# Retention with key blocks of 128, 128, 128, 112 and 32: the last block's three products of high and low parts stacked into one contraction of 96 rows

## The chip, the cores and the metric

The kernel runs on one core of one Trainium2 chip. The metric is the device time of one execution in microseconds (us), of which the median of three runs is given. TensorE (PE) does the matmuls, and PEld is its weight load; VectorE (DVE) and ScalarE (ACT) move and split numbers; GpSimd (POOL) and SyncE (SP) issue most of the transfers.

## The reference, cut to what matters

A decoder of two layers: each is a half-step SwiGLU block, a mixer, and another half-step SwiGLU block, on 16 learned tokens and 512 inputs (528 positions of width 1024). The mixer of layer 0 is retention with four heads, keys of 256 and values of 512:

```
q = rotary(q); k = rotary(k) * 256 ** -0.5
scores = einsum('bhid,bhjd->bhij', qi, ki) * decay_intra      # inside a chunk of 64
o = einsum('bhij,bhjv->bhiv', scores, vi) + einsum('bhid,bhdv->bhiv', qi * decay_q, S)
S = S * decay_chunk + einsum('bhjd,bhjv->bhdv', ki * decay_k, vi)
o = rmsnorm(o, head_norm) * silu(g)
return o @ w_out
```

Everything is in float32. The kernel computes the recurrence as one triangular product over all 528 positions: the decay is folded into the tables that turn q and k, so that scores times values with a causal mask gives the same o.

## The kernel before, in words

A float32 product is made of three matmuls. Each operand is split into a high part, rounded for the fast float32 matmul (fp32r), and a low part, which is what the rounding left. `mm3` (L397) issues high x high, high x low and low x high into one accumulator; these are the lines L398, L399 and L400 of the profile. Weights stream in by DMA and are split as they arrive: ACT makes the high part (`whi`, L159), DVE the low part (`wlo`, L160). `unit` steps do the projections, with three names of accumulators (`X..`, `QZ..`, `su..`).

Retention (`retention`, L1072) goes head by head (h = 0 to 3). After the projections of queries, keys and values, the positions are cut along the keys into NJ = 5 blocks of widths JW, 128 four times and 16. For each block j, `steps` calls two functions:

- `score(j)`: the scores of the block's keys against all later queries. The keys of the block are the matmul's weights (128 x JW), the queries are what streams past, for two halves m of the key width: 6 matmuls per block (12 for block 0, which goes in two segments). DVE multiplies the diagonal square by the causal mask (L1241), and ACT and DVE split the scores into `ph` and `pl` (L431, L432).
- `turn(j)`: four transposes on PE bring the values of the block (`vt`) into a PSUM bank `tv`, keys on partitions (L1221); ACT and DVE split them into `vh` and `vl` (L431 and L432, and L550 and L551 in head 0, where they are scaled as well).

`pv` (L1273) multiplies: for each of four value slices m an accumulator `po` collects `mm3` of every block j, with the block's values as the weights (JW rows, 128 columns) and its scores streaming. Block 4 of `po` has 16 contraction rows and 16 streaming columns. Afterwards ACT squares `po` (L1292) and DVE takes it into the gate (L1326) or, in head 3, into `ob` (L1346). Two `po` are in use at a time (pool `acc`, two buffers); scores of blocks 0 to 3 use the same pool. `tv`, the scores of block 4 and the accumulators `X..` share a ring of four banks.

In heads 0 to 2 two gate units (`Xrg..`) stand between `steps` and `pv`; in head 3 `pv` follows `steps` directly. What stands in which order on an engine is set by a scheduler that reorders by its own estimates; the engines then run their rows strictly in that order, and a row whose input is not there holds up all that stand behind it on its engine.

Of the kernel before, what the change touches and what calls it, by code (L numbers as in the profile page):

```python
# [10 lines left out]
F32 = mybir.dt.float32  # L11
F32R = mybir.dt.float32r
# [4 lines left out]
P = 128  # L17
# [5 lines left out]
MR = 32  # L23
T = 528
# [18 lines left out]
NMASK = 5  # L43

NJ = 5
JW = (128, 128, 128, 128, 16)
PO = (0, 528, 928, 1200, 1344, 1360)


BY_JT = ((0, 128, 4, 512), (512, 16, 1, 16))  # L50
# [167 lines left out]
def trunk(ctx, tc, a):  # L218
    nc = tc.nc
    V, S, G = nc.vector, nc.scalar, nc.gpsimd  # L220

    const = ctx.enter_context(tc.tile_pool(name="const", bufs=1))
# [129 lines left out]
    ident = const.tile([P, P], F32, name="ident")  # L352
    nc.sync.dma_start(ident, a["tri"][0])
    causal = const.tile([P, P], F32, name="causal")
    nc.sync.dma_start(causal, a["tri"][1])
    ones_r = const.tile([P, P], F32R, name="ones")
    V.memset(ones_r.bitcast(F32), 1.0)
    ones = ones_r.bitcast(F32)
# [12 lines left out]
    rb = upool.tile([P, T], F32, tag="rb", name="rb")  # L371
# [13 lines left out]
    def hook():  # L385

        W.fetch()
        if pend:
            pend[0][0] -= 1
            if pend[0][0] <= 0:  # L390
                pend.popleft()[1]()
# [5 lines left out]
    def mm3(ps, lh, ll, rh, rl, start, stop, **kw):  # L397
        nc.tensor.matmul(ps, lhsT=lh, rhs=rh, start=start, stop=False, **kw)  # L398
        nc.tensor.matmul(ps, lhsT=lh, rhs=rl, start=False, stop=False, **kw)  # L399
        return nc.tensor.matmul(ps, lhsT=ll, rhs=rh, start=False, stop=stop, **kw)  # L400
# [9 lines left out]
    def acc_tile(name):  # L410
        other["turn"] += 1
        if other["banks"] == 2 and other["turn"] % 3 == 0:
            return other["pool"].tile([P, 2, 512], F32, tag="acc", name=name)
        return acc.tile([P, 2, 512], F32, tag="acc", name=name)

    def bank(name):
        if other["ring"]:
            other["ring"].rotate(-1)
            return other["pool"].tile([P, 512], F32, tag=other["ring"][-1], name=name)
        return other["pool"].tile([P, 512], F32, tag="bank", name=name, bufs=other["banks"])  # L420
# [9 lines left out]
    def split(hi, lo, src):  # L430
        S.copy(hi, src)  # L431
        V.tensor_sub(lo, src, hi.bitcast(F32))  # L432
# [116 lines left out]
    def split_scaled(hi, lo, src, by_row):  # L549
        S.activation(hi, src, AF.Copy, scale=by_row)  # L550
        V.scalar_tensor_tensor(lo, src, by_row, hi.bitcast(F32), ALU.mult, ALU.subtract)  # L551
# [520 lines left out]
    def retention(feed):  # L1072
        with tc.tile_pool(name="retp", bufs=1) as rp, tc.tile_pool(name="wmore", bufs=2) as wp, psum_pool(4) as pp:
# [40 lines left out]
            def head(h):  # L1114
                qk = {}
# [64 lines left out]
                vt, sgs, v, sc_parts = [], [], [], []  # L1180
# [34 lines left out]
                def turn(j):  # L1215
                    if not v:
                        v.extend(rp.tile([P, NJ, RDV], F32R, tag="v" + i, name=f"v{i}{h}") for i in "hl")
                    j0, jw = j * P, JW[j]
                    tv = bank(f"tv{h}{j}")
                    for m in range(4):  # L1220
                        nc.tensor.transpose(tv[:jw, m * P:(m + 1) * P], vt[m][:, j0:j0 + jw], ident)  # L1221
                    if h == 0:
                        split_scaled(v[0][:jw, j, :], v[1][:jw, j, :], tv[:jw, :], rc[:jw, j:j + 1])
                    else:
                        split(v[0][:jw, j, :], v[1][:jw, j, :], tv[:jw, :])

                def score(j):

                    if not sc_parts:
                        sc_parts.extend(rp.tile([P, PO[-1]], F32R, tag="p" + i, name=f"p{i}{h}") for i in "hl")  # L1230
                    j0, jw = j * P, JW[j]
                    sc = acc_tile(f"sc{h}{j}") if j < NJ - 1 else bank(f"sc{h}{j}").unsqueeze(1)
                    segs = HALVES if j == 0 else ((j0, T),)
                    n = segs[0][1] - segs[0][0]
                    for b, (i0, i1) in enumerate(segs):
                        for m in range(2):
                            kh, kl = qk["k", m]
                            qh, ql = qk["q", m]
                            mm3(sc[:jw, b, :n], kh[:, j0:j0 + jw], kl[:, j0:j0 + jw], qh[:, i0:i1], ql[:, i0:i1],
                                m == 0, m == 1)  # L1240
                    V.tensor_mul(sc[:jw, 0, :jw], sc[:jw, 0, :jw], causal[:jw, :jw])  # L1241
                    dst = [t[:jw, PO[j]:PO[j + 1]].rearrange("p (b t) -> p b t", b=len(segs)) for t in sc_parts]
                    split(dst[0], dst[1], sc[:jw, :len(segs), :n])

                def steps():
                    for j in range(NJ):
                        score(j)
                        turn(j)
# [24 lines left out]
                def pv(into):  # L1273

                    sqs = tmp.tile([P, T], F32, tag="sqa", name=f"osq{h}", bufs=1)
                    for m in range(4):
                        po = acc_tile(f"po{h}{m}")
                        for j in range(NJ):
                            j0, jw = j * P, JW[j]
                            for hf, (r0, r1) in enumerate(((0, P), (P, T))):  # L1280
                                i0 = max(r0, j0)
                                if i0 >= r1:
                                    continue
                                c = slice(PO[j] + i0 - j0, PO[j] + r1 - j0)
                                mm3(po[:, hf, i0 - r0:r1 - r0], v[0][:jw, j, m * P:(m + 1) * P],
                                    v[1][:jw, j, m * P:(m + 1) * P], sc_parts[0][:jw, c], sc_parts[1][:jw, c],
                                    j == 0, j == (NJ - 1 if hf else 0))
                        hook()
                        t = sqs if m == 0 else tmp.tile([P, T], F32, tag="sg", name=f"osq{h}{m}")
                        for hf, r in enumerate(((0, P), (P, T))):  # L1290
                            o = po[:, hf, :r[1] - r[0]]
                            S.activation(t[:, r[0]:r[1]], o, AF.Square)  # L1292
                            into(m, o, r)
                        if m:
                            V.tensor_add(sqs, sqs, t)
                    return sqs
# [23 lines left out]
                if h < RH - 1:  # L1320
# [4 lines left out]
                    def into(m, o, r):  # L1325
                        V.scalar_tensor_tensor(sgs[m][:, r[0]:r[1]], o, gain(m), sgs[m][:, r[0]:r[1]],  # L1326
                                               ALU.mult, ALU.mult)

                    sqs = pv(into)
                    result()  # L1330

# [8 lines left out]
                else:  # L1340
# [4 lines left out]
                    def into(m, o, r):  # L1345
                        V.tensor_scalar(ob[m][:, r[0]:r[1]], o, gain(m), None, ALU.mult)  # L1346

                    sqs = pv(into)
                    result()

# [696 lines left out]
```

## Time and profile before

| | |
|---|---|
| median of 3 runs | 2074.59 us (2074.48 to 2075.45) |
| span of the profiled execution | 2072.5 us |
| PE busy | 2061.5 us, 99% |
| DVE busy | 1789.9 us, 86% |
| ACT busy | 1192.8 us, 58% |
| POOL busy | 209.3 us, 10% |
| granted TensorE clock, mean | 0.999 |

The profile gives a span, from the first instruction to the last, and not the time of the same execution with what lies around it: the median of the runs is 2.1 us above this span. In rows of the timeline the columns are start, duration of one or of a merged group, engine, line, operation, and output from inputs. PE rows overlap, since matmuls are pipelined: what a matmul costs is the distance from its start to the start of the next one, not its duration. A form such as 16\*128 16x16 is a weight tile of 16 rows and 128 columns and an operand of 16 rows that streams 16 columns.

### The profile page before, as it was taken

Reading aid. Unit: us, or ns where it says so; the run is one execution under the profiler, and the core shown is the slowest. Engines: PE = TensorE matmul, PEld = TensorE weight load, DVE = VectorE, ACT = ScalarE, POOL = GpSimd, SP = SyncE. Lnnn points to the kernel's source line nnn. Section 1 sums busy time; section 2 is a strip of 40 time slices with the busy share of each in tenths; the row PEclk is TensorE's granted clock in tenths of the full one; section 3 lists DMA queues with packets and bytes.
Section 4 is the critical chain, followed back from the end, with each engine's and each line's share of the span. In section 5 each row is a group of like instructions: output and inputs, shape, how many; then the busy total and the mean of one; then the engine's idle time right before and its main releaser. Section 6 shows DMA issues by size and latency. Waiting matters only on the chain. (4 is left out here: it accounts for less than half of the span.)

```text
span 2072.5 us, 42971 instructions
## 1 busy us (share of the span) xinstructions
PE 2061.5 (99%) x16367; PEld 2016.6 (97%) x16367; DVE 1789.9 (86%) x3214; ACT 1192.8 (58%) x2330; POOL 209.3 (10%) x181
## 2 busy tenths in 40 slices
PE   9999999999999999999999999999999999999998
PEld 9999999999999999999999999999999988999998
DVE  8989889968686879988889998889997968998886
ACT  5656566554545455656566565666655445666664
POOL 1011111010101000111111011110101000111110
PEclk9999999999999999999999999999999999999999
DMA  7676767354554531776776376676614341686762
GB/s 223 159 190 162 193 179 193 98 144 132 144 133 131 142 101 67 183 188 161 187 194 179 107 180 181 151 208 172 200 57 117 93 162 60 166 210 175 183 178 72
DMA packets 176111, 318.84 MB, mean 154 GB/s; under 512 B 17568, under 2 KB 40736, under 8 KB 175904
## 3 DMA queue, kind: packets, MB, share of 16 engines
q1 hardware_dynamic: 133856, 237.04, 34.0%
q0 software_dynamic: 40896, 75.51, 22.4%
q10 hardware_dynamic: 1152, 3.55, 0.5%
q8 instruction: 128, 2.10, 0.4%
q14 instruction: 79, 0.65, 0.1%
HBM read 311.76 MB, written 4.26 MB: 152 GB/s over the span
## 5 line engine op out<-in xcount | busy, mean ns | idle before, releaser
L159 ACT CAST whi<-raw 128x512 fp32r<-128x512 f32 (+1 forms) x893 | 526.0, 606 | 484.3 <-DVE raw L165 97.3
L160 DVE TENSOR_TENSOR wlo<-raw,whi 128x512 fp32r<-128x512 f32 (+1 forms) x893 | 583.8, 669 | 143.4 <-ACT whi L159 136.1
L159 ACT CAST whi<-pair 128x512 fp32r<-128x512 f32 (+1 forms) x304 | 183.5, 604 | 119.5 <-PE Xf11u L399 7.3
L160 DVE TENSOR_TENSOR wlo<-pair,whi 128x512 fp32r<-128x512 f32 (+1 forms) x304 | 202.0, 665 | 7.0 <-ACT whi L159 5.6
L128 POOL DMA_DIRECT2D pair<-in_f_in x73 | 88.5, 1213 | 720.7 <-DVE wlo L160 338.7
L165 DVE TENSOR_TENSOR raw<-pair,raw 128x512 f32<-128x512 f32 (+1 forms) x146 | 97.3, 667 | 2.6
L167 DVE TENSOR_TENSOR raw<-raw,raw 128x512 f32<-128x512 f32 (+1 forms) x146 | 97.2, 666 | 2.4
L128 POOL DMA_DIRECT2D pair<-in_f_out x44 | 53.2, 1208 | 380.4 <-DVE wlo L160 133.6
L399 PE MATMUL po_r<-ogl,whi 128*128 128x264 f32 x256 | 72.7, 284 | 0.0
L398 PE MATMUL po_r<-ogh,whi 128*128 128x264 f32 x256 | 72.6, 283 | 0.0
L400 PE MATMUL po_r<-ogh,wlo 128*128 128x264 f32 x256 | 72.5, 283 | 0.0
L128 POOL DMA_DIRECT2D pair<-in_ret_in x20 | 24.3, 1216 | 297.2 <-DVE wlo L160 144.3
L398 PE MATMUL Xf20o<-hf,whi 128*128 128x264 f32 x176 | 50.9, 289 | 0.2
L398 PE MATMUL Xf11o<-hf,whi 128*128 128x264 f32 x176 | 50.9, 289 | 0.2
L398 PE MATMUL Xf10o<-hf,whi 128*128 128x264 f32 x176 | 50.8, 289 | 0.2
L399 PE MATMUL Xf10o<-hf,whi 128*128 128x264 f32 x176 | 50.0, 284 | 0.0
L399 PE MATMUL Xf11o<-hf,whi 128*128 128x264 f32 x176 | 50.0, 284 | 0.0
L399 PE MATMUL Xf20o<-hf,whi 128*128 128x264 f32 x176 | 50.0, 284 | 0.0
L400 PE MATMUL Xf20o<-hf,wlo 128*128 128x264 f32 x176 | 49.9, 285 | 0.0
L400 PE MATMUL Xf11o<-hf,wlo 128*128 128x264 f32 x176 | 49.9, 285 | 0.0
L400 PE MATMUL Xf10o<-hf,wlo 128*128 128x264 f32 x176 | 49.9, 285 | 0.0
L400 PEld LDWEIGHTS po_r<-ogh,wlo 128*128 128x128 f32 x256 | 48.2, 188 | 0.0
(987 smaller groups left out, 8523.9 us busy)
## 6 DMA issues: line engine op xcount, KB each, us to landing
raw<-in_f_in SPq DMA_DIRECT2D x277, 256.0 KB, 4.4
pair<-in_f_in SPq DMA_DIRECT2D x150, 256.0 KB, 4.7
pair<-in_f_in POOLq DMA_DIRECT2D x73, 512.0 KB, 6.4
raw<-in_f_out SPq DMA_DIRECT2D x80, 256.0 KB, 3.7
raw<-in_ret_in SPq DMA_DIRECT2D x76, 256.0 KB, 3.0
raw<-in_f_out SPq DMA_DIRECT2D x72, 192.0 KB, 3.0
pair<-in_f_out SPq DMA_DIRECT2D x48, 256.0 KB, 3.8
pair<-in_f_out POOLq DMA_DIRECT2D x24, 512.0 KB, 5.8
```

The costliest lines, as they stand in the source:

```text
L128: nc.gpsimd.dma_start(t, aps[2].unsqueeze(1).broadcast_to([P, 2, n]), accum_op=ALU.add)
L159: self.nc.scalar.copy(hi[:, :n], raw)
L160: V.tensor_sub(lo[:, :n], raw, hi[:, :n].bitcast(F32))
L165: V.tensor_add(s2, self.tiles[c][:, 1], self.tiles[c, "a11"])
L167: V.tensor_add(raw, raw, s2)
L398: nc.tensor.matmul(ps, lhsT=lh, rhs=rh, start=start, stop=False, **kw)
L399: nc.tensor.matmul(ps, lhsT=lh, rhs=rl, start=False, stop=False, **kw)
L400: return nc.tensor.matmul(ps, lhsT=ll, rhs=rh, start=False, stop=stop, **kw)
```

## The change

The blocks become 128, 128, 128, 112 and 32 wide. In the last block the 32 keys are written three times, so that high x high, low x high and high x low lie beside each other on 96 rows, and one matmul of 96 contraction rows does what three did. To fill the rows:

- at the start ACT copies three 32x32 squares of the causal mask into `ctail`;
- for the scores ACT copies the last 32 keys of each half three times side by side (`krh`, `krl`, one buffer each), so that the 6 matmuls of block 4 have 96 weight columns and stream 32; DVE multiplies 96 rows by `ctail`, ACT rounds all 96 rows into `ph`, DVE overwrites the middle 32 with the low part;
- for the values ACT copies the last 32 positions of each `vt` three times (`vr`, two buffers for four copies), four transposes of 96 columns follow, ACT rounds 96 rows into `vh` and DVE overwrites the last 32 with the low part; in head 0 DVE first scales the 32 positions in place by `rb` (four small products), in place of the scaling inside the split;
- in `pv` block 4 is one matmul of 96 rows and 32 columns for each m.

```diff
-JW = (128, 128, 128, 128, 16)
-PO = (0, 528, 928, 1200, 1344, 1360)
+JW = (128, 128, 128, 112, 32)
+PO = (0, 528, 928, 1200, 1344, 1376)
+J4 = T - MR
...
+    ctail = const.tile([3 * MR, MR], F32, name="ctail")
+    for g in range(3):
+        S.copy(ctail[g * MR:(g + 1) * MR], causal[g * MR:(g + 1) * MR, g * MR:(g + 1) * MR])
...
+                    if j == NJ - 1:
+                        n = 3 * MR
+                        for m in range(4):
+                            if h == 0:
+                                V.tensor_mul(vt[m][:, J4:], vt[m][:, J4:], rb[:, J4:])
+                            rows = rp.tile([P, 3, MR], F32, tag=f"vr{m % 2}", name=f"vr{h}{m}")
+                            S.copy(rows, vt[m][:, J4:].unsqueeze(1).broadcast_to([P, 3, MR]))
+                            nc.tensor.transpose(tv[:n, m * P:(m + 1) * P], rows.rearrange("p g i -> p (g i)"), ident)
+                        hi = v[0][:n, j, :]
+                        S.copy(hi, tv[:n])
+                        V.tensor_sub(hi[2 * MR:], tv[2 * MR:n], hi[2 * MR:].bitcast(F32))
+                        return
...
-                    sc = acc_tile(f"sc{h}{j}") if j < NJ - 1 else bank(f"sc{h}{j}").unsqueeze(1)
+                    if j == NJ - 1:
+                        n = 3 * MR
+                        sc = bank(f"sc{h}{j}")[:n, :MR]
+                        for m in range(2):
+                            kr = [rp.tile([P, 3, MR], F32R, tag=f"kr{i}", name=f"kr{i}{h}{m}") for i in "hl"]
+                            for t, k in zip(kr, qk["k", m]):
+                                S.copy(t, k[:, J4:].bitcast(F32).unsqueeze(1).broadcast_to([P, 3, MR]))
+                            kr = [t.rearrange("p g i -> p (g i)") for t in kr]
+                            qh, ql = qk["q", m]
+                            mm3(sc, *kr, qh[:, J4:], ql[:, J4:], m == 0, m == 1)
+                        V.tensor_mul(sc, sc, ctail)
+                        pm = sc_parts[0][:n, PO[j]:PO[j + 1]]
+                        S.copy(pm, sc)
+                        V.tensor_sub(pm[MR:2 * MR], sc[MR:2 * MR], pm[MR:2 * MR].bitcast(F32))
+                        return
+                    sc = acc_tile(f"sc{h}{j}")
...
+                            if j == NJ - 1:
+                                nc.tensor.matmul(po[:, 1, J4 - P:T - P], lhsT=v[0][:3 * MR, j, m * P:(m + 1) * P],
+                                                 rhs=sc_parts[0][:3 * MR, PO[j]:PO[j + 1]], start=False, stop=True)
+                                break
```

Three places in the order of rows show it. In the names the digits behind `sc`, `tv`, `po` and `vr` are the head and the block (or m), and a row's `[waits ..]` names the engines whose signal it needs.

PE, head 0, from the scores of block 4 on, before (the rows left out are further matmuls of the same tile):

```order
L398 MATMUL sc04_5680<-q00_0_5147,k00_0_5301 16x16 [waits DVE_49]
...
L398 MATMUL sc02_5646<-q00_0_5147,k00_0_5301 128x272 [waits DVE_49]
...
L1221 MATMUL tv04_5690<-ident_111,vt00_5326 16x128 [waits DVE_49]
L1221 MATMUL tv04_5690<-ident_111,vt01_5394 16x128
L1221 MATMUL tv04_5690<-ident_111,vt02_5457 16x128
L1221 MATMUL tv04_5690<-ident_111,vt03_5524 16x128
L398 MATMUL Xrg00_5699<-uha_131,whi242_5351 128x264 [waits DVE_49]
...
L398 MATMUL sc03_5663<-q00_0_5147,k00_0_5301 128x144 [waits DVE_49]
```

The same place after:

```order
L402 MATMUL sc04_5684<-q00_0_5151,krh00_5685 96x32 [waits DVE_49]
...
L402 MATMUL sc02_5650<-q00_0_5151,k00_0_5305 128x272 [waits DVE_49]
...
L1231 MATMUL tv04_5702<-ident_111,vr00_5704 96x128 [waits DVE_49]
L1231 MATMUL tv04_5702<-ident_111,vr01_5708 96x128 [waits Activation_49]
L402 MATMUL sc04_5684<-q01_0_5160,krh01_5692 96x32 [waits Activation_49]
L403 MATMUL sc04_5684<-q11_0_5161,krh01_5692 96x32
L404 MATMUL sc04_5684<-q01_0_5160,krl01_5693 96x32 [waits Activation_49]
L402 MATMUL Xrg00_5723<-uha_135,whi242_5355 128x264 [waits DVE_49,PE_49]
...
L402 MATMUL sc03_5667<-q00_0_5151,k00_0_5305 112x144 [waits DVE_49]
...
L1231 MATMUL tv04_5702<-ident_111,vr02_5712 96x128 [waits Activation_49]
L1231 MATMUL tv04_5702<-ident_111,vr03_5716 96x128 [waits Activation_49]
```

The second half of block 4's scores and of its transposes has moved back, each behind a copy on ACT, and other matmuls stand in front of it.

ACT, head 0, the rows that feed these, after:

```order
L435 CAST ph0_5606<-sc01_5633 128x400 [waits DVE_49]
L1254 CAST krh01_5692<-k01_0_5316 128x96 [waits PE_49]
L435 CAST ph0_5606<-sc02_5650 128x272 [waits DVE_49]
L1254 CAST krl01_5693<-k11_0_5317 128x96
L1260 CAST ph0_5606<-sc04_5684 96x32 [waits DVE_49]
L1230 COPY vr02_5712<-vt02_5461 128x96 [waits DVE_49,PE_49]
L1230 COPY vr03_5716<-vt03_5528 128x96 [waits DVE_49,PE_49]
L1233 CAST vh0_5624<-tv04_5702 96x512 [waits PE_49]
L435 CAST ph0_5606<-sc03_5667 112x144 [waits DVE_49]
```

Before, this stretch of ACT held five rows:

```order
L431 CAST ph0_5602<-sc01_5629 128x400 [waits DVE_49]
L550 ACTIVATE vh0_5620<-tv04_5690,rc_134 16x512 [waits PE_49,Pool_49]
L431 CAST ph0_5602<-sc02_5646 128x272 [waits DVE_49]
L431 CAST ph0_5602<-sc04_5680 16x16 [waits DVE_49]
...
L431 CAST ph0_5602<-sc03_5663 128x144 [waits DVE_49]
```

The copies of the second half stand between the roundings of the scores; those of the first half are done many rows earlier.

PE, head 0, in `pv` the end of the first `po` and the start of the second, before:

```order
L399 MATMUL po00_5972<-pl0_5603,vh0_5620 128x144
L400 MATMUL po00_5972<-ph0_5602,vl0_5621 128x144
L398 MATMUL po00_5972<-ph0_5602,vh0_5620 128x16
L399 MATMUL po00_5972<-pl0_5603,vh0_5620 128x16
L400 MATMUL po00_5972<-ph0_5602,vl0_5621 128x16
L398 MATMUL po01_5995<-ph0_5602,vh0_5620 128x128 [waits DVE_49]
```

And after:

```order
L403 MATMUL po00_5996<-pl0_5607,vh0_5624 128x144
L404 MATMUL po00_5996<-ph0_5606,vl0_5625 128x144
L1312 MATMUL po00_5996<-ph0_5606,vh0_5624 128x32
L402 MATMUL po01_6017<-ph0_5606,vh0_5624 128x128 [waits DVE_49]
L403 MATMUL po01_6017<-pl0_5607,vh0_5624 128x128
```

Three rows have become one, 16 times in all (four m, four heads), and nothing else moves there.

More of the change, by code (lines that the diff above doesn't have):

```diff
@@ L1286, in pv @@
                                     v[1][:jw, j, m * P:(m + 1) * P], sc_parts[0][:jw, c], sc_parts[1][:jw, c],
-                                    j == 0, j == (NJ - 1 if hf else 0))
+                                    j == 0, not hf)
                         hook()
```

## The prediction

> **What bounds the kernel now.** I read the first page first, then the waits of PE inside retention, then PE's timeline row by row.
>
> ```profile
> span 2072.5 us, 42971 instructions
> PE 2061.5 (99%) x16367; PEld 2016.6 (97%) x16367; DVE 1789.9 (86%) x3214; ACT 1192.8 (58%) x2330; POOL 209.3 (10%) x181
> ...
> PEclk9999999999999999999999999999999999999999
> ```
>
> PE is busy 99% of the span at full clock, so a microsecond of PE time saved or added anywhere is a microsecond of the kernel, unless PE then waits. In retention (390 to 750 us) it hardly waits:
>
> ```profile
> PE sc L398 <- DVE pl L432: 0.3, 1, 0.3
> PE po L398 <- DVE pl L432: 0.2, 1, 0.2
> ```
>
> These are its only listed waits there. So two numbers decide: PE time that the stacked matmuls save, and new waits of PE for copies on ACT.
>
> **The gain in `pv`.** PE in head 0, at the end of one `po` and the start of the next (start, duration, ...):
>
> ```profile
> 434.28 0.28 PE L400 MATMUL po<-ph,vl 128*128 128x144 f32 x1
> 434.48 0.27 PE L398 MATMUL po<-ph,vh 16*128 16x16 f32 x1
> 434.62 0.25 PE L399 MATMUL po<-pl,vh 16*128 16x16 f32 x1
> 434.73 0.25 PE L400 MATMUL po<-ph,vl 16*128 16x16 f32 x1
> 434.91 0.33 PE L398 MATMUL po<-ph,vh 128*128 128x128 f32 x1
> 435.07 0.28 PE L399 MATMUL po<-pl,vh 128*128 128x128 f32 x1
> ```
>
> From the last matmul of block 3 to the second of the next `po` pass 435.07 - 434.28 = 0.79 us: steps of 0.20, 0.14, 0.11, 0.18, 0.16. The three 16-row matmuls thus cost more than their number: the steps into them, out of them and after are wider. What would one matmul of 96 rows cost there? The other mixer has one in the same position:
>
> ```profile
> 1562.51 0.28 PE L400 MATMUL go<-PF,v 128*128 128x128 f32 x1
> 1562.62 0.45 PE L1836 MATMUL go<-PM,v 96*128 96x512 f32 x1
> 1562.91 0.39 PE L398 MATMUL go<-PF,v 128*128 128x512 f32 x1
> ```
>
> The step into it is 0.11, that of any 128-column weight tile with little to stream, with no widening. Its step out, 0.29, is for 512 columns, and 32 columns can't need more than the weight load, 0.11. So I take three steps of 0.11 = 0.33 in place of 0.79: 0.46 less for each of 4 m x 4 heads, 16 x 0.46 = 7.4 us. Upper end: the step after is shorter still, 0.51 x 16 = 8.2. Lower end: the widened steps stay with one matmul, and only 0.14 + 0.11 go, 16 x 0.25 = 4.0. I stay with 7.4, since the row of 96 rows is the nearest one.
>
> Here two rules of the Trainium skill disagree about size. TensorEngine Tiling (Array Packing), Tiling Modes, says that a change of tiling mode drains TensorE, and its Performance Considerations tie four-way row tiling to a contraction of 32; 96 rows would be no tiling, both drains go, and the result is the forecast's. TensorE: Matmul & The Clock Gate, LDWEIGHTS, says that a weight load takes time by its columns and not by its contraction rows; by that alone block 4 would merely go from three loads to one, the second rival's direction. The 0.20 into 16 rows against 0.11 into 96 speaks for the first.
>
> **The cost in the scores: wider weights.** Head 1, block 4 and block 3:
>
> ```profile
> 514.71 0.17 PE L399 MATMUL sc<-q,k 128*16 128x16 f32 x1
> 514.74 0.17 PE L400 MATMUL sc<-q,k 128*16 128x16 f32 x1
> ...
> 514.84 0.60 PE L1221 MATMUL tv<-ident,vt 128*16 128x128 f32 x4
> 515.19 0.37 PE L398 MATMUL Xrg<-uha,whi 128*128 128x264 f32 x1
> ...
> 515.83 0.28 PE L399 MATMUL sc<-q,k 128*128 128x144 f32 x1
> 515.94 0.28 PE L400 MATMUL sc<-q,k 128*128 128x144 f32 x1
> ```
>
> A matmul with 16 weight columns steps 0.026 (0.03 as rounded), one with 128 steps 0.11. By columns 96 should step 0.086: 6 x 0.06 = 0.36 more per head, 1.4 in all; at 0.11 it would be 6 x 0.084 = 0.50, 2.0 in all; at no growth 0. I take 1.4. The same page's LDWEIGHTS formula (columns divided by 1.2, in ns) would give 80 against 13 ns, an estimate of 24 x 0.067 = 1.6 us. The transposes step about 0.11 with 16 columns ((0.60 - 0.27) / 3 in a merged row whose last one lasts 0.27), as with 128: nothing changes at 96. Block 3 with 112 keys streams the same 144 columns: nothing.
>
> **The cost in the scores: new waits.** The buffers `krh`, `krl` are single, so the copies for m = 1 wait for the matmuls of m = 0, and stand in ACT's queue behind roundings of scores, which wait for DVE. Head 0 before, from PE, ACT and DVE:
>
> ```profile
> 410.26 0.29 PE L400 MATMUL sc<-q,k 128*128 128x272 f32 x1
> ...
> 411.05 0.39 PE L398 MATMUL Xrg<-uha,whi 128*128 128x264 f32 x1
> ...
> 410.36 0.51 ACT L431 CAST ph<-sc 128x400 fp32r<-128x400 f32 x1
> ...
> 411.71 0.39 ACT L431 CAST ph<-sc 128x272 fp32r<-128x272 f32 x1
> 412.79 0.16 ACT L431 CAST ph<-sc 16x16 fp32r<-16x16 f32 x1 [0.69 <-DVE sc L1241]
> ...
> 409.59 1.40 DVE L551 SCALAR_TENSOR_TENSOR vl<-tv,rc,vh 128x512 fp32r<-128x512 f32 x2
> 410.91 0.57 DVE L432 TENSOR_TENSOR pl<-sc,ph 128x400 fp32r<-128x400 f32 x1
> ...
> 411.59 0.74 DVE L551 SCALAR_TENSOR_TENSOR vl<-tv,rc,vh 128x512 fp32r<-128x512 f32 x1
> 412.24 0.43 DVE L432 TENSOR_TENSOR pl<-sc,ph 128x272 fp32r<-128x272 f32 x1
> ```
>
> A copy of 96 columns isn't in the trace; it lies between a 16x16 rounding (0.16) and the 272-wide one (0.39), I take 0.2, nearest the small end. PE issues block 2 until 410.39, two transposes until 410.61, and then needs `krh01`: ACT has it at 410.36 + 0.51 + 0.2, about 411.1. The third matmul needs `krl01`, behind the 272-wide rounding: 411.1 + 0.39 less overlap + 0.2, about 411.55. So `Xrg` starts near 411.7 instead of 411.05, 0.63 later. Then PE comes, at about 413.2, to the transposes of `vr02`; that copy needs DVE's in-place scaling, which stands behind block 2's mask product (possible from 410.26 + 0.29 on, 0.2), `vl` 0.74, `pl` 0.57, `pl` 0.43, `vl` 0.74 and the small mask product 0.2, about 413.3 with 0.1 of overlap between rows; the copy ends near 413.5: a wait of 0.4, and 0.22 for the two transposes, which stood ahead of `Xrg` before. Head 0: 1.25 us, of which 0.36 is the wider weights. Heads 1 to 3 have no such scaling:
>
> ```profile
> 514.88 1.17 ACT L431 CAST vh<-tv 128x512 fp32r<-128x512 f32 x2 [0.51 <-PE tv L1221]
> ...
> 723.74 0.40 ACT L431 CAST ph<-sc 128x272 fp32r<-128x272 f32 x1
> ...
> 724.76 0.30 PE L398 MATMUL po<-ph,vh 128*128 128x128 f32 x1 [0.23 <-DVE pl L432]
> ```
>
> In head 1 (and 2) `krh11` follows the first of the two roundings at 514.88, done near 515.4, copied by 515.6; PE comes for it after three `Xrg` matmuls at 515.5: 0.15, with the wider weights 0.5. In head 3 the copies follow the row at 723.74, ready at 724.3 and 724.5; PE gets there at 724.1 and waits 0.4, but it waited 0.23 before `po` anyway: 0.25 in all. Block 4's `vh` (copy and low part of 32 rows) would end near 727.1, about when PE comes to it. Sum on this side: 1.25 + 2 x 0.5 + 0.25 = 2.5 us, bounds 1.4 (no waits) and 7 (each head like head 0 with half as much again).
>
> **What may take some of it back.** A `po` buffer is reused two m later, after ACT and DVE have emptied it:
>
> ```profile
> 437.45 0.25 PE L400 MATMUL po<-ph,vl 16*128 16x16 f32 x1
> ...
> 438.97 0.63 DVE L1326 SCALAR_TENSOR_TENSOR gs<-po,gains,gs 128x400 f32<-128x400 f32 x1 [0.57 <-ACT osq L1292]
> ...
> 440.35 0.33 PE L398 MATMUL po<-ph,vh 128*128 128x128 f32 x1
> ```
>
> DVE ends at 439.60, the buffer is taken at 440.35: 0.75 to spare, of which a faster round takes 0.46 and an end that lies later by 0.07 and a signal of 0.1 more: 0.1 left. I charge 0.3 for all heads; at worst 8 x 0.2 = 1.6.
>
> The three copies of `ctail` cost nothing: the mask's transfer is issued at 10.9 us, ACT does them between early weight splits, and ACT then idles 1.36 us for a transfer:
>
> ```profile
> L355 SPq DMA_DIRECT2D causal<-in_tri x1: 328/328/328, 10.9 to 10.9; - x1
> ...
> 20.32 1.25 ACT L159 CAST whi<-raw 128x512 fp32r<-128x512 f32 x2 [1.36 <-DMA raw<-in_f_in]
> ```
>
> Without that cover they would cost three small copies, some 0.4. ACT's other new copies (8 per head, about 6 us in all) lie in an engine idle 42% of the time, and DVE's few products likewise; the split weights PE needs stay ahead. No transfer moves, on SP's queue or POOL's.
>
> **Sum.** -7.4 + 2.5 + 0.3 = -4.6 us. The profiled span of 2072.5 would become 2067.9; with the 2.1 us that the median of the runs lies above it, 2074.6 - 4.6 = 2070.0 us.
>
> **Rivals.**
> 1. Forecast: the wide steps around 16 rows go, waits of about 1 us. 2068.0 to 2072.0, likeliest 2070.0.
> 2. The wide steps stay with 96 rows: -4.0 + 2.5 = -1.5, 2073.1 us. For it: no row here has 96 rows with only 32 columns. Against: 0.11 at 1562.62.
> 3. `pv` becomes bound by emptying `po`, or the waits are twice mine: -7.4 + 1.6 + 4 = -1.8, 2072.8 us. For it: only 0.1 to spare, and a copy price that is an estimate.
> 4. Slower: in every head PE stands behind ACT's queue for both `krh`/`krl` and `vr`. With two full roundings of 0.59 before each copy, that is 2 x (2 x 0.59 + 0.2) = 2.8 per head, 11 in all, with wider weights 12.5: +5, about 2080. It decides once waits pass 7.4 - 1.4 + 4.2 = 10.2 us. Against: by the ACT rows PE is 0.15 to 0.6 early, not 1.4.
>
> That the change doesn't do what it says isn't likely: one row stands where three stood, 16 times.
>
> **Chances.** A comparison can tell about 0.2% from no change, 4.15 us. Forecast 0.70, rival 2 0.12, rival 3 0.13, rival 4 0.05. The forecast's own spread crosses 0.2% at 2070.4: 0.54 of its 0.70 lies below. So faster 0.54, same 0.41, slower 0.05. The range reaches below to 16 x 0.51 saved with hardly a wait (2067.6) and above over rivals 2 and 3 to 2073.5.
>
> **What the profile after would show.** The step from block 3's last matmul to the second of the next `po` near 0.33 instead of 0.79; `sc` with 128\*96 stepping 0.09; a wait of PE for `krh`, `krl` or `vr` on ACT of 0.3 to 0.5 in head 0 and under 0.2 in heads 1 and 2. I am wrong if the step into 96\*128 is 0.2, if PE's waits on ACT in retention pass 3 us, or if PE waits for DVE at the third and fourth `po`.

## The result, and the profile after

The changed kernel takes 2070.89 us (median of 17 runs, 2069.56 to 2073.86) against 2074.82 us; the ratio is 0.9982, 95% interval 0.9975 to 0.9989, or 3.9 us less. A second series, on another occasion, gave 2070.11 us against 2074.74 (0.9979, 0.9970 to 0.9988). Predicted were 2070.0 us and a range of 2067.6 to 2073.5. The prediction gave a chance of 0.54 to a fall of more than 0.2%; the two series lie on either side of that, at 0.18% and 0.21%. The profiled execution took 2071.41 us, 1.8 above its span.

The page of the changed kernel; PE is as full as before, with 32 matmuls fewer:

```profile
span 2069.6 us, 42946 instructions
PE 2057.5 (99%) x16335; PEld 2012.9 (97%) x16335; DVE 1790.8 (87%) x3218; ACT 1200.2 (58%) x2365; POOL 208.8 (10%) x181
```

The lines that answer to those of `pv`: PE's timeline in head 0, from block 3's last matmul to the second of the next `po` (start, duration, ...).

```profile
436.31 0.28 PE L404 MATMUL po<-ph,vl 112*128 112x144 f32 x1
436.42 0.22 PE L1312 MATMUL po<-ph,vh 96*128 96x32 f32 x1
436.49 0.31 PE L402 MATMUL po<-ph,vh 128*128 128x128 f32 x1
436.63 0.27 PE L403 MATMUL po<-pl,vh 128*128 128x128 f32 x1
```

436.63 - 436.31 = 0.32 us where it was 0.79: steps of 0.11, 0.07 and 0.14. The wide steps are gone.

The same engine in head 0's scores, then ACT (in brackets: idle time before, and what ended it):

```profile
411.73 0.26 PE L402 MATMUL sc<-q,krh 128*96 128x32 f32 x1 [0.28 <-ACT krh L1254]
411.83 0.24 PE L403 MATMUL sc<-q,krh 128*96 128x32 f32 x1
412.19 0.26 PE L404 MATMUL sc<-q,krl 128*96 128x32 f32 x1
...
414.26 0.49 PE L1231 MATMUL tv<-ident,vr 128*96 128x128 f32 x2 [0.38 <-ACT vr L1230]
```

```profile
411.37 0.31 ACT L1254 CAST krh<-k 128x96 fp32r<-128x96 f32 x1
411.56 0.40 ACT L435 CAST ph<-sc 128x272 fp32r<-128x272 f32 x1
411.84 0.29 ACT L1254 CAST krl<-k 128x96 fp32r<-128x96 f32 x1
```

PE waits 0.28 for `krh`; `krl` follows a 272-wide rounding, and the third product starts 0.36 after the second where 0.085 would be its step; then 0.38 for `vr`. In head 3 the last of the four transposes of `vr` falls inside `pv`: two `po` matmuls are out, and 0.35 us later, where their step would be 0.11, comes the transpose.

```profile
723.45 0.28 PE L403 MATMUL po<-pl,vh 128*128 128x128 f32 x1
723.80 0.31 PE L1231 MATMUL tv<-ident,vr 128*96 128x128 f32 x1
```

To see where the time went, retention is cut at PE's rows: from a head's first `sc` to its first `po` (scores, transposes, gates), from there to the first matmul behind `pv`, and from there to the next head's first `sc` (the stretch with the next head's `rqk`, `out` and `rv`). The rows that mark this in head 0, first of before, then of after:

```profile
404.44 0.29 PE L398 MATMUL sc<-q,k 128*128 128x264 f32 x1
...
432.30 0.22 PE L398 MATMUL po<-ph,vh 128*128 128x128 f32 x1
...
443.07 0.39 PE L398 MATMUL Xrqkq<-uha,whi 128*128 128x264 f32 x1
...
509.27 0.28 PE L398 MATMUL sc<-q,k 128*128 128x264 f32 x1
```

```profile
405.33 0.28 PE L402 MATMUL sc<-q,k 128*128 128x264 f32 x1
...
434.33 0.22 PE L402 MATMUL po<-ph,vh 128*128 128x128 f32 x1
...
443.21 0.37 PE L402 MATMUL Xrqkq<-uha,whi 128*128 128x264 f32 x1
...
509.63 0.28 PE L402 MATMUL sc<-q,k 128*128 128x264 f32 x1
```

The differences are 27.86, 10.77 and 66.20 us before, 29.00, 8.88 and 66.42 after. Read in the same way in every head and every kernel that follows, each from its one profiled execution (us; the last column runs from the first `sc` of head 0 to the end of head 3's `pv`):

| kernel | scores, heads 0 to 3 | pv, heads 0 to 3 | stretches 0-1, 1-2, 2-3 | all |
|---|---|---|---|---|
| before | 27.86, 27.21, 27.20, 6.93 | 10.77, 10.76, 10.77, 10.86 | 66.20, 66.19, 66.43 | 331.18 |
| after | 29.00, 27.66, 27.65, 6.98 | 8.88, 8.87, 8.87, 9.32 | 66.42, 66.82, 66.83 | 327.30 |
| after_again | 29.00, 27.65, 27.64, 6.98 | 8.88, 8.87, 8.88, 9.32 | 66.41, 67.01, 66.83 | 327.47 |
| three96 | 29.02, 27.65, 27.64, 6.98 | 9.77, 9.78, 9.78, 10.21 | 67.42, 67.85, 67.00 | 333.10 |
| rows32 | 28.99, 27.65, 27.66, 6.99 | 9.88, 9.89, 9.88, 10.31 | 66.44, 66.42, 66.84 | 330.95 |
| rows64 | 29.01, 27.64, 27.65, 6.98 | 9.87, 9.87, 9.87, 10.29 | 66.45, 66.47, 66.85 | 330.95 |
| hihi16 | 27.80, 27.21, 27.20, 6.94 | 9.84, 9.84, 9.84, 9.96 | 66.13, 67.05, 66.60 | 328.41 |
| bufs | 28.51, 27.82, 27.81, 6.92 | 8.88, 8.88, 8.87, 8.96 | 66.39, 67.06, 66.83 | 326.93 |
| copyfirst | 28.50, 27.83, 27.81, 6.93 | 8.88, 8.88, 8.88, 8.98 | 66.41, 66.41, 68.09 | 327.60 |
| early1 | 28.07, 27.82, 27.83, 6.93 | 8.87, 8.88, 8.87, 8.95 | 66.47, 66.65, 66.85 | 326.19 |
| padA | 27.90, 27.19, 27.20, 6.94 | 10.72, 10.72, 10.72, 10.80 | 66.77, 66.50, 66.68 | 332.14 |
| padAB | 27.93, 27.21, 27.20, 6.93 | 10.72, 10.71, 10.72, 10.80 | 66.68, 66.50, 66.65 | 332.05 |
| place | 28.94, 27.64, 27.64, 6.99 | 8.85, 8.85, 8.85, 9.26 | 66.21, 67.13, 66.59 | 326.95 |
| early1_place | 28.27, 27.85, 27.82, 6.94 | 8.85, 8.85, 8.84, 8.90 | 66.21, 66.11, 66.59 | 325.23 |

After against before: scores +2.09, `pv` -7.22, stretches +1.25, together -3.88 us. The span fell by 2.9 only, since PE was 0.89 us late at head 0's first `sc` in this profile, and needed 0.1 more behind head 3's `pv`. The 1.25 stands in no term of the prediction; most of the experiments' later part is about it.

### The profile page after: what moved, and what is told of

It is laid out like the page before. It is cut to its first block, busy times and chain, and to the rows that moved or that the text cites. A ratio compares the mean times of both kernels' runs of the same rounds, so it can differ in the third digit from the quotient of the medians.

```text
span 2069.6 us, 42946 instructions
## 1 busy us (share of the span) xinstructions
PE 2057.5 (99%) x16335; PEld 2012.9 (97%) x16335; DVE 1790.8 (87%) x3218; ACT 1200.2 (58%) x2365; POOL 208.8 (10%) x181
## 4 chain that ended last, share of the span: by engine, by line
PE 95%; DVE 2%; ACT 1%; issue 1%; DMA 0%; POOL 0%; SPq 0%; POOLq 0%; ACTq 0%; DVEq 0%
PE po_r L403 2%; PE po_r L402 2%; PE po_r L404 2%; PE Xf20o L402 1%; PE Xf10o L402 1%; PE Xf11o L402 1%; PE Xf10o L404 1%; PE Xf10o L403 1%; PE Xf20o L403 1%; PE Xf20o L404 1%; PE Xf11o L403 1%; PE Xf11o L404 1%; PE lv L1614 1%; PE Xf20u L402 1%; PE Xf11u L402 1%; PE Xf21u L404 1%
## 5 line engine op out<-in xcount | busy, mean ns | idle before, releaser
L402 PEld LDWEIGHTS po_r<-ogh,whi 128*128 128x128 f32 x256 | 48.3, 189 | 0.0
```

## Experiments

Times are medians with their ratio to the kernel before, timed beside it. They come from several series: three96, hihi16, rows32 and bufs were timed in one, rows64, early1, copyfirst and after_again in the next, with 9 to 11 runs each, and the kernels that move buffers in later ones. Differences of 1 us and less between them are read from the table, not from the medians.

**What makes the steps wide: the number of matmuls or their rows?** Three matmuls of 96 rows:

```diff
-  nc.tensor.matmul(po[:, 1, J4 - P:T - P], lhsT=v[0][:3 * MR, ...], rhs=sc_parts[0][:3 * MR, ...], start=False, stop=True)
+  for i in range(3):
+      nc.tensor.matmul(po[:, 1, J4 - P:T - P], lhsT=v[0][:3 * MR, ...], rhs=sc_parts[0][:3 * MR, ...], start=False, stop=i == 2)
```

> The changed kernel with its one 96-row matmul per po issued three times (block 4's products are added three times). Theory (the gaps around block 4 came with the 16 contraction rows, not with the number of matmuls): two more 96-row matmuls cost two plain steps of 0.09 to 0.11 us, so from block 3's last matmul to the second of the next po 0.50 to 0.55 us instead of 0.32; 16 x 0.18 to 0.22 = +2.9 to +3.5 us, 2073.3 to 2074.4 us. Rival (every short matmul brings wide steps of 0.14 to 0.2, whatever its rows): 0.65 to 0.75 us, +5.5 to +7 us, 2076.4 to 2078.

2076.26 us (ratio 1.0009, 1.0000 to 1.0018). PE's timeline in head 0 (the row of 96\*128 merges three matmuls):

```profile
436.15 0.28 PE L404 MATMUL po<-ph,vl 112*128 112x144 f32 x1
436.26 0.45 PE L1313 MATMUL po<-ph,vh 96*128 96x32 f32 x3
...
436.70 0.27 PE L403 MATMUL po<-pl,vh 128*128 128x128 f32 x1
```

0.55 us, 0.23 more for two matmuls: the theory's step, and no gap. The time came near the rival's, though: of the 5.80 us by which retention is longer than in the changed kernel, 3.6 are in `pv` and 2.2 in the stretches. Of these, 0.9 are waits of PE for copies that have nothing to do with `pv` (the other 1.3 were not taken apart):

```profile
PE QZrqkk L402 <- ACT surqkk L614: 0.9, 2, 0.7
...
565.63 0.62 ACT L160 CAST whi<-raw 128x512 fp32r<-128x512 f32 x1 [1.50 <-DMA raw<-in_ret_o]
```

ACT's queue holds the rounding of a weight that is still being loaded, 1.5 us of idle time, and behind it the copy `surqkk` that PE needs.

The opposite edit, the kernel before with one matmul of 16 rows where three stood:

```diff
+  if j == NJ - 1:
+      nc.tensor.matmul(po[...], lhsT=v[0][:jw, j, ...], rhs=sc_parts[0][:jw, c], start=False, stop=True)
+      continue
   mm3(po[...], v[0][:jw, j, ...], v[1][:jw, j, ...], sc_parts[0][:jw, c], sc_parts[1][:jw, c], ...)
```

> The kernel before with only the high x high matmul of block 4 in pv (leaves out the two products with low parts of the last 16 keys): one 16-row matmul where three stood. Theory (the wide steps stay around one matmul of 16 rows): only the steps of 0.14 and 0.11 us go, from block 3's last matmul to the second of the next po 0.54 us, 16 x 0.25 = -4.0 us, of which up to 0.6 is waited for later: 2070.8 to 2071.5. Rival (the number of matmuls is the price): 0.30 to 0.36 us as with one of 96 rows, -7 us, of which some 1 is waited for later: 2067.5 to 2069.

2072.24 us (0.9992, 0.9983 to 1.0001).

```profile
434.95 0.28 PE L400 MATMUL po<-ph,vl 128*128 128x144 f32 x1
435.16 0.27 PE L1286 MATMUL po<-ph,vh 16*128 16x16 f32 x1
435.36 0.33 PE L398 MATMUL po<-ph,vh 128*128 128x128 f32 x1
435.52 0.27 PE L399 MATMUL po<-pl,vh 128*128 128x128 f32 x1
```

One matmul of 16 rows takes 0.57 us of passage, as much as three of 96: steps of 0.21, 0.20 and 0.16 remain. The theory holds on the step; of the 3.7 us saved in `pv` 1.0 went into the stretches (PE waited 0.67 for `surqkk` in the second one), more than the 0.6 I had allowed, and the time lies above the theory's 2070.8 to 2071.5.

**Where do the wide steps begin?** The stacked matmul with fewer rows:

```diff
-  lhsT=v[0][:3 * MR, ...], rhs=sc_parts[0][:3 * MR, ...]
+  lhsT=v[0][:MR, ...], rhs=sc_parts[0][:MR, ...]            # rows64: 2 * MR
```

> The changed kernel with the stacked matmul of pv restricted to its first 32 contraction rows (leaves out the two products with low parts for the last 32 keys). Theory (a contraction of 32 rows or fewer, as one of 16, makes the steps into it and out of it wide): the passage from block 3's last matmul to the second of the next po takes 0.50 to 0.58 us instead of 0.32, +2.9 to +4 us, 2073.5 to 2074.9. Rival (the gaps of before came from three matmuls in a row or from 16 columns, rows don't matter): 0.32 us, 2070.9, no change.

> The changed kernel with the stacked matmul of pv restricted to its first 64 contraction rows (leaves out the product of low values by high scores for the last 32 keys). 32 rows gave 0.58 us from block 3's last matmul to the second of the next po, 96 rows 0.32. Theory (only a contraction of 32 rows or fewer makes wide steps): 0.32 to 0.34 us, 2070.4 to 2071.4. Rival (64 rows or fewer do): 0.5 to 0.58 us, 2073.3 to 2074.5.

2074.00 us (0.9998, 0.9989 to 1.0007) with 32 rows, 2074.37 us (0.9999, 0.9990 to 1.0007) with 64. PE's timeline of the two, 32 rows first (its two rows in between are left out):

```profile
435.57 0.28 PE L404 MATMUL po<-ph,vl 112*128 112x144 f32 x1
...
436.15 0.28 PE L403 MATMUL po<-pl,vh 128*128 128x128 f32 x1
```

```profile
436.00 0.28 PE L404 MATMUL po<-ph,vl 112*128 112x144 f32 x1
436.21 0.28 PE L1312 MATMUL po<-ph,vh 64*128 64x32 f32 x1
436.42 0.33 PE L402 MATMUL po<-ph,vh 128*128 128x128 f32 x1
436.58 0.27 PE L403 MATMUL po<-pl,vh 128*128 128x128 f32 x1
```

0.58 us in both. With two thirds of the contraction the matmul costs 0.26 us more than with all of it, and nearly the whole gain of the change is gone. My theory for 64 rows fell: the border lies between 64 and 96 rows, not at 32. In the Trainium skill, TensorEngine Tiling (Array Packing), Performance Considerations, a contraction of 64 goes with two-way and one of 32 with four-way row tiling; with the drain on a change of mode (Tiling Modes) these rules fit all four sizes, if such matmuls count as tiled, which no row here says. I had used the four-way case alone.

The weight loads show where the time goes, in rows64 and then in the changed kernel:

```profile
436.21 0.18 PEld L1312 LDWEIGHTS po<-ph,vh 64*128 64x128 f32 x1
```

```profile
436.35 0.19 PEld L1312 LDWEIGHTS po<-ph,vh 96*128 96x128 f32 x1
```

With 64 rows the load starts 0.21 us behind the start of block 3's last matmul (436.00), together with its own matmul; with 96 rows it starts 0.04 behind (436.31), beside the matmul before it. The 0.20 to 0.21 stand in all 16 places of before, hihi16 and rows32 too, and the 0.04 to 0.05 in all 16 of the changed kernel. So a load is not overlapped where a tile of 64 rows or fewer follows one of 112 or more. On the way out it is the same: in rows64 the next `po`'s first load starts with its matmul, at 436.42. What holds the load back no row tells.

**The waits in the scores.** The same kernel with copies in buffers of their own, then also earlier in the program:

```diff
-  kr = [rp.tile([P, 3, MR], F32R, tag=f"kr{i}", ...) for i in "hl"]
+  kr = [v[1][:, j, (2 * m + i) * n:(2 * m + i + 1) * n].rearrange("p (g i) -> p g i", g=3) for i in range(2)]
-  rows = rp.tile([P, 3, MR], F32, tag=f"vr{m % 2}", ...)
+  rows = rp.tile([P, 3, MR], F32, tag=f"vr{m}", ...)
```

> The changed kernel with buffers of their own for the copies of both m (the krh/krl copies in the unused last block of vl, four vr buffers instead of two); nothing is left out. Theory (PE's waits in the scores come from the single krh/krl and double vr buffers, which put the second copies behind roundings in ACT's queue): PE's waits for krh and krl go (0.28 and about 0.25 us in head 0, 0.15 in heads 1 and 2, 0.24 and 0.2 in head 3), the 0.38 for vr in head 0 shrinks, together -1.0 to -1.5 us, 2069.4 to 2070.0. Rival (ACT's queue itself is late, or what PE gains is waited for at the next weights): 2070.5 to 2071.2, no change.

2070.05 us (0.9979, 0.9971 to 0.9988). PE's waits between 380 and 750 us (total, times, longest):

```profile
PE Xrg L402 <- ACT surg L616: 0.5, 3, 0.2
PE Xrqkk L402 <- ACT surqkk L620: 0.4, 1, 0.4
PE sc L402 <- DVE pl L436: 0.3, 1, 0.3
PE tv L1231 <- ACT vr L1230: 0.3, 1, 0.3
```

No wait for `krh` or `krl` is left; the one for `vr` is still 0.3. Head 0 gains 0.49, head 3 0.4; heads 1 and 2 lose 0.16 each, which I had not expected: with other buffers the rows come in another order, and `Xrg` waits three times for `surg`. The table's last column is 0.4 to 0.5 us under the two profiles of the changed kernel, short of the theory's 1.0 to 1.5; the median is 0.8 under the first series of the changed kernel and no better than the second (2070.11), so the time alone shows no gain. The early copies:

```diff
   for j in range(NJ):
       score(j)
       turn(j)
+      if j == 1:
+          copies()          # krh, krl, vr of all m; head 0: vr = vt * rb in one product on DVE
```

> The kernel with buffers of its own for the copies, and all eight copies of a head are written behind block 1's scores, head 0's vr by one product on DVE instead of an in-place product and a copy; nothing is left out. Theory (the copies are late only because of where they stand in ACT's queue): PE waits neither for the copies of k nor for vr, and against 2070.05 us the 0.26 for vr and 0.3 for pl in head 0 shrink: 2069.4 to 2069.9. Rival (the copies now stand ahead of roundings that PE's later matmuls need): a wait of 0.2 to 0.5 per head for ph or pl at the first po, 2070.5 to 2071.5.

2069.25 us (0.9975, 0.9965 to 0.9985). Between 380 and 750 us PE waits neither for `krh`, `krl` nor for `vr`; the list is:

```profile
PE sc L402 <- DVE pl L436: 0.3, 1, 0.3
PE Xrg L402 <- ACT surg L616: 0.3, 2, 0.2
PE Xrg L402 <- DVE vl L555: 0.2, 1, 0.2
```

The theory holds: 0.93 us of head 0's 1.14 are back. What is left of the scores' growth, 0.21 + 0.61 + 0.63 us, has no such wait in it. In heads 1 and 2 it is mostly the wider weights (the six matmuls of block 4 take 0.29 us more than in before) and the wait for `surg` (the `QZrg` matmuls take 0.34 to 0.36 more).

**The stretches, first try: the late weight.** A scheduling constraint puts the roundings of weights behind the three `surqkk` copies:

```diff
+  if moved:                  # steps a11, s1, s2 of rqkk
+      W.after = done         # the surqkk copy; roundings from here on are issued behind it
+      hook()
```

> The kernel with buffers of its own for the copies (2070.05 us), and in heads 0 to 2 the roundings of weights that ACT did ahead of the three surqkk copies stand behind them; nothing is left out. Theory (part of what pv gains is waited for at Xrqkk and QZrqkk, because ACT's queue has the rounding of a weight of in_ret_o, still on its way, ahead of the surqkk copy that PE waits for): the wait of PE for surqkk in head 1 (0.35 us in the changed kernel, 0.4 with buffers of its own) goes, and the time falls by 0.3 to 0.6 us, to 2069.4 to 2069.8. Rival (PE needs that late weight itself soon after, so the wait moves to po_r): the surqkk wait goes, an equal one for whi stands within 3 us behind it, 2070.0.

2070.76 us (0.9981, 0.9972 to 0.9989): no gain over 2070.05. Stretch 1-2 fell to 66.41 us without a wait, as in the theory, but in 2-3 another wait came up:

```profile
PE po_r L406 <- DVE wlo L163: 1.2, 1, 1.2
```

That is the rival, one head further on: a weight that is rounded later is itself waited for, by more than was gained.

**The stretches, second try: nothing of `pv`, but where the buffers lie.** In rows32 and rows64, with a slow `pv` and no listed wait of PE in the stretches, they are longer all the same, 66.4, 66.4 and 66.8 us. Of this, 0.23 in each stretch is spread over `po_r`'s 192 matmuls: the first sixty take 7.33 instead of 7.26 us, all of them 23.49 instead of 23.26 (in stretch 0-1 from 465.56 in before to the next row, `Xrv` at 488.82, and from 465.66 to 489.15 in after). The change puts 128 bytes per partition (`ctail`) ahead of nearly all buffers, and widens both score buffers by 64, so that what lies behind them (`vh`, `vl`, `ogh`, `ogl`) moves by 256. The kernel before, with unused space alone; the order of PE's instructions is the same row by row:

```diff
+  room = const.tile([P, MR], F32, name="room")
-  rp.tile([P, PO[-1]], F32R, tag="p" + i, ...)
+  rp.tile([P, PO[-1] + 16], F32R, tag="p" + i, ...)
+  nc.gpsimd.memset(rp.tile([P, 3, MR], F32, tag=f"room{i}", ...), 0.0)     # padAB only, four times
```

> The kernel before with unused space only: 128 bytes per partition ahead, 64 more in each score buffer, and 1536 behind, so that all buffers of retention and of its extra weights lie where the changed kernel has them; the order of PE's instructions is that of before, nothing is left out. What is asked: the stretches between one head's pv and the next head's scores take 66.42 to 66.47, 66.42 to 67.85 and 66.83 to 67.00 us in every kernel with the stacked products, whatever its pv costs, and 66.20, 66.19 and 66.43 us before; in them po_r's matmuls step 0.122 instead of 0.121 us. Theory (where the buffers lie sets that step): 66.42, 66.4 and 66.8 us here too, +0.9 us with the last head's out, about 2075.5. Rival (the other engines' traffic, moved by the changed order, sets it): 66.2, 66.2 and 66.4 us, no change, 2074.6.

> The kernel before with 256 bytes of unused space (128 ahead of retention's buffers, 64 in each score buffer), without the 1536 bytes behind: ogh and ogl lie as in the changed kernel, the extra weights' buffers 256 bytes on instead of 1792. Theory (the place of ogh and ogl, what the matmuls of po_r stream, matters): gaps of 66.42, 66.4, 66.8 us. Second theory (the place of the weights matters): 66.20, 66.19 and 66.43 us here, and longer ones only with the 1536 bytes. Rival (no place matters): as before in both.

2075.64 us with all of it (1.0004, 0.9995 to 1.0013, in which a difference of 0.9 us can't be told); padA had one run, 2077.17 us, of which 2.3 are a late start. So the profile decides: the stretches are 66.68, 66.50 and 66.65 us (padAB) and 66.77, 66.50 and 66.68 us (padA), 1.0 and 1.1 us more than before. The group of `po_r`'s matmuls on the first product (least/middle/longest ns), in before, after and padA:

```profile
L398 PE MATMUL po_r<-ogh,whi x256: 278/284/289, 465.6 to 781.4; 128*128 128x264 f32 x128
```

```profile
L402 PE MATMUL po_r<-ogh,whi x256: 279/285/291, 465.7 to 778.5; 128*128 128x264 f32 x128
```

```profile
L400 PE MATMUL po_r<-ogh,whi x256: 279/285/291, 468.1 to 784.8; 128*128 128x264 f32 x128
```

With unused bytes alone, before gets the rows of after: `po_r` takes 23.49 us in each stretch of padA and padAB, 0.7 more in all than in before. The other 0.3 to 0.4 us of their growth, most of it in stretch 0-1, is not in after and stays unexplained. The 1536 bytes behind, which move only the extra weights' buffers, change nothing in `po_r`. The reverse, the changed kernel and early1 with the buffers where before has them:

```diff
-  ctail = const.tile([3 * MR, MR], F32, name="ctail")
+  ctail.append(rp.tile([3 * MR, 2 * MR], F32, tag="ctail", name="ctail")[:, :MR])   # behind retention's other buffers, filled by GpSimd
-  sc_parts.extend(rp.tile([P, PO[-1]], ...) for i in "hl")
+  sc_parts.extend(rp.tile([P, PO[n]], ...) for i, n in (("h", NJ), ("l", NJ - 1)))
```

> The changed kernel with its buffers put back where the kernel before has them: ctail lies behind retention's other buffers and is filled by GpSimd in head 0, and the low half of the scores ends at column 1344, since nothing reads block 4 there; order and work of PE as in the changed kernel, nothing is left out. Theory (256 bytes of shift make po_r's matmuls step 0.122 instead of 0.121 us): the stretches between the heads take 66.2, 66.2 to 66.8 and 66.4 us instead of 66.42, 66.82 and 66.83, pv perhaps 0.05 us per head more (it took 0.05 less when the kernel before was shifted), -0.6 to -0.9 us in all: 2069.6 to 2070.1. Rival (the changed kernel's own traffic lengthens them too): 66.4, 66.8 and 66.8 us, 2070.7.

> The fastest kernel so far (eight copies early in buffers of their own, 2069.25 us) with its buffers put back where the kernel before has them; nothing is left out. Theory (the two gains are of different places and add up): stretches of 66.2, 66.2 to 66.6 and 66.4 us, scores of 28.1, 27.8 and 27.8 us as without it, 2068.3 to 2068.7. Rival (PE then only waits for ACT and DVE sooner): stretches as in the changed kernel, 2069.2.

2069.57 us (0.9976, 0.9967 to 0.9985) and 2068.64 us (0.9971, 0.9960 to 0.9983; 7 runs), the fastest of all, 6.0 us under before. In place's `po_r` and waits:

```profile
L400 PE MATMUL po_r<-ogh,whi x256: 278/284/289, 465.6 to 778.0; 128*128 128x264 f32 x128
...
PE Xrqkk L400 <- ACT surqkk L618: 0.8, 1, 0.8
```

The step is the old one, and stretches 0-1 and 2-3 fall by 0.21 and 0.24 us; 1-2 is hidden behind the longest `surqkk` wait seen here, 0.8. early1_place, without that wait, has 66.21, 66.11 and 66.59 us against early1's 66.47, 66.65 and 66.85: -1.06, the whole of its gain of 0.96 in the table; 0.7 of it is `po_r`, back at 23.26 us in each stretch. The medians, whose intervals overlap with those of the kernels not put back, would not show this by themselves.

**The start.** 

> The changed kernel once more. Theory (PE's first microseconds depend on when the first transfers land, which differs from run to run: the profiles at 10 us stand 0.0 or 0.7 to 0.9 us behind that of before, without regard to the edits): the profile starts either like before or 0.7 to 0.9 later, pv takes 7.4 to 7.6 us less than before and the scores 2.4 to 2.6 more in either case, and the median lies within 2070.4 to 2071.4. Rival (the three ctail copies delay the start): 0.9 us late in this profile too, and in every kernel that has them.

2070.11 us. Its profile is 0.28 us late at head 0's first `sc`, with the same `ctail` copies; the first one was 0.89 late, early1 0.56, rows32 0.17, and hihi16, which has none of them, 0.74. So the copies don't set it, and the start is not one of two values, as I had put it, but anything between 0 and 0.9 us, in padA more; the rest of the theory holds, except that this median lies 0.3 below its bounds. What PE waits for there is the first weights. ACT in the first profile of the changed kernel:

```profile
6.47 0.62 ACT L160 CAST whi<-raw 128x512 fp32r<-128x512 f32 x1 [1.25 <-DMA raw<-in_f_in]
```

## Why the prediction was right, and where not

- **`pv`, -7.4 us: right.** The passage measures 0.32 against 0.33 (in steps of 0.11, 0.07 and 0.14 rather than three of 0.11), and `pv` is shorter by 7.22 us with head 3's wait and transpose of `vr` in it (some 0.37, against early1). The reason given, that the wide steps belong to few contraction rows and not to small matmuls, is shown by three96, hihi16, rows32 and rows64. Rival 2 (2073.1 us) is out for 96 rows; with 64 its wide steps stay, at 2074.37 us.
- **Wider weights, +1.4 us: the right step, the sum a little too high.** `sc` with 96 columns steps 0.085 (predicted 0.086). In head 1, where bufs has no wait among them, the six matmuls of block 4 take 0.53 us (513.76 to 514.29) against 0.24 in before (514.60 to 514.84): 0.29 a head, about 1.2 in all, since the first of the six steps 0.11 in both. Block 3 with 112 keys steps 0.10 instead of 0.11 and gives back 0.06 a head, which I had put at nothing. Weight loads grouped by form, between 400 and 440 us (total us, mean ns of one):

```profile
L402 PEld LDWEIGHTS sc<-q,k 128*128 128x128 f32 x8 | 1.5, 188 | 0.3 <-DVE pl L436 0.3
...
L402 PEld LDWEIGHTS sc<-q,krh 128*96 128x96 f32 x2 | 0.3, 160 | 0.5 <-ACT krh L1254 0.5
```

  28 ns less for 32 columns less agrees with columns divided by 1.2, the rule of the Trainium skill in TensorE: Matmul & The Clock Gate, LDWEIGHTS (26.7 by it, an estimate). The durations themselves, 188 and 160 ns, are some 80 longer than by that rule.
- **New waits, +1.1 us: right in size, and in place but for head 3.** Head 0 grew by 1.14 (predicted 1.25, weights included), heads 1 and 2 by 0.45 each (0.5), head 3 by 0.05 in the scores and about 0.37 in `pv` (0.25): 2.46 against 2.5 us, weights included. In head 3 I had expected the wait at `krh`; it is there (0.24), but the wait for `pl` ahead of `po` goes in exchange, and the cost is in `pv`, at the transposes of `vr`, for which I had charged nothing there. The copies of k take 0.29 to 0.31 us in their rows rather than 0.2. bufs and early1 take these waits away, and the table's last column follows (326.93 and 326.19 us). Rival 4 was far off.
- **Emptying `po`, +0.3 us: nothing.** PE has no wait for a `po` buffer in the list. In head 0 DVE empties it by 440.79 and PE takes it at 440.97, 0.18 later, where I had 0.1 left; the 0.1 that I charged for the signal is too much, since PE starts 0.05 behind the copy of `krh` that it waits for (411.37 + 0.31 = 411.68, and 411.73).

```profile
440.15 0.64 DVE L1361 SCALAR_TENSOR_TENSOR gs<-po,gains,gs 128x400 f32<-128x400 f32 x1 [0.57 <-ACT osq L1327]
```

- **What failed: the step "a microsecond of PE time saved or added anywhere is a microsecond of the kernel, unless PE then waits".** The sum costs the edit where it stands and puts everything behind it at nothing; 1.25 us came back in the stretches between the heads. The rows account for it. In each of the three stretches `po_r` takes 0.23 us more, 0.7 in all. That is no wait but longer steps of matmuls that the edit leaves as they were, and it is the shift of the buffers, which the diff shows as three numbers and one small tile, and which place and early1_place undo. In stretch 1-2, 0.4 is the wait for `surqkk` behind a late weight (66.82 against the 66.44 of rows32 and rows64). In stretch 2-3 there is another wait of 0.4, of which 0.16 is left once PE's gains just before it are counted: in after DVE has the low part of a weight ahead of `rtq`, which PE's weight load needs, where before has it behind (`rtq` at 661.05, the low part at 661.39).

```profile
658.88 0.68 DVE L161 TENSOR_TENSOR wlo<-raw,whi 128x512 fp32r<-128x512 f32 x1
659.49 0.42 DVE L1131 TENSOR_TENSOR rtq<-Xrqkq,surqkq 128x264 f32<-128x264 f32 x1
...
659.96 0.19 PEld L402 LDWEIGHTS Xrqkq<-rth,whi 128*128 128x128 f32 x1 [0.44 <-DVE rtq L1131]
```

  hihi16 and early1_place have this wait too, so neither the stacked matmul nor the place of the buffers makes it; it goes with the order of rows on DVE.
- **Luck in the total.** `pv` and the scores together gave 5.1 us where the sum had 4.9, and the 0.3 for emptying `po` did not come. Both made up for part of the 1.25 that the sum had left out: without them the total would have missed by that 1.25, not by 0.7.
- **What stays open.** When the late weight lands varies: the `surqkk` wait was nothing in before and rows32, 0.3 to 0.4 in after, after_again and bufs, 0.67 to 0.8 in hihi16 and place, 0.9 in three96, where PE was later and not earlier. So it isn't simply that PE now comes sooner; what sets it wasn't found. Nor was it tried which of the moved buffers makes the matmuls slower: all behind the constants moved by 128 bytes, and those named by 256. Most other matmuls of that form, `QZf20u` for one, step as in before (0.1219 us in before, after and padA), so the shift doesn't touch all alike. And `pv` became 0.05 us per head shorter when before was shifted, but not longer when the changed kernel was put back.

## What to carry to other kernels

Look at the contraction rows of a small remainder before counting its matmuls: on this chip's trace one matmul of 16, 32 or 64 rows among matmuls of 128 cost 0.25 us more than one of 96, so a small remainder is worth stacking to 96 rows if the copies that it takes cost less. Sizes between 64 and 96 were not tried. Copies that feed such a stack need buffers of their own and an early place in the queue of the engine that makes them; that was worth about 1 us here (326.19 against 327.30 and 327.47 us in the table). And where a change is worth a few microseconds, compare the addresses of the buffers before and after: a constant of 128 bytes and two score buffers wider by 64 each moved what lies behind them and took back some 0.7 us in the three stretches.

## What the hardware showed that I had not expected

- The same matmuls, in the same order and with the same shapes, step 0.1210 or 0.1222 us in `po_r`, according to where their buffers lie (7.26 us for sixty in before and place, 7.33 in after, rows32 and padA).
- A contraction of 64 rows has the wide steps of 16 and 32 (0.58, 0.57 and 0.58 us); one of 96 has none (0.32). In the rows, the weight load of the former starts 0.20 to 0.21 us behind the start of the matmul before it, that of the latter 0.04.
- The first microseconds differ between runs, by 0 to 2.3 us at head 0's first `sc`, with the landing of the first weights; one profile's span is therefore no measure of an edit worth a few microseconds, while its inner stretches repeat within 0.02 us between after and after_again, but for 1-2, where the wait for `surqkk` lies.
